# Value projections in another order with fewer loads, and weighted sums of 512 queries, in an encoder trunk

## The chip, the cores and the metric

The program runs on one core of one Trainium2 chip. The metric is the device time of one execution in microseconds; the median of several executions is compared. One execution was also taken with the hardware profiler.

## The reference

Two groups of 512 tokens (`x_prompt`, `x_sample`, 1024 wide) go through the same two layers and a final norm. All is float32.

```python
def trunk(x, ...):
    for i in range(DEPTH):                       # 2
        h = rms_norm(x, norm_g[i], NORM_EPS)
        if i % 2 == 0:
            x = x + diff_attention(h, ...)
        else:
            x = x + bidir_retention(h, ...)
    return rms_norm(x, final_norm_g, NORM_EPS)

def diff_attention(h, w_in, ..., w_out, lambda_init):
    q, k, v, gate = split(h @ w_in)              # 2048 each
    # 16 heads of 128 for q and k, rotated; 8 heads of 256 for v
    p = softmax(q k^T)                           # per head of 128, 512 x 512
    a = p[:, :, 0] - lam * p[:, :, 1]            # two score maps for each head of v
    o = rms_norm(a v, subln_g) * (1 - lambda_init)
    return (o * silu(gate)) @ w_out

def bidir_retention(h, w_in, decay_fwd, decay_bwd, subln_g, w_out):
    q, k, v, gate = split(h @ w_in)              # 1024, 1024, 2048, 2048; 8 heads
    o = retention(q, k, v, forward) + retention(q, k, v, backward)
    return (rms_norm(o, subln_g) * silu(gate)) @ w_out
```

## The kernel before

**Numbers.** Each operand of a matrix product is split in a high part (ACT casts it, `hi_of`, L557) and a low part (DVE subtracts, `lo_of`, L560). A product is three passes (`PASSES`): high by high, high by low, low by high.

**Projections.** Both groups are projected together by a seven-product scheme of the Strassen-Winograd kind: the products P1 to P7 need sums and differences of the four quarters of a block of weights, x(i, k) with i the half of the columns and k the half of the rows, and of the activations (`Bop`, made once a layer by `make_b`). A `Unit` does one head of q, k or gate: 12 matrix products for each of P1 to P7, from two loads of weights. A `Double` does four heads of v at once: each of P1 to P7 is 48 matrix products of 512 columns on four banks, and its weights come in two parts (kh = 0, 1). There are two Doubles in each layer. `prep` loads weights into the ring `raw` (four places of 512 KB), combines them on DVE (L874, into the ring `st`, three places) and writes high and low parts into the ring `ws` (seven places). `product` runs on PE (L909; a `Unit`'s is L775). `evac` takes finished banks away, with copies on ACT (`copies`) or sums on DVE (`sums`, L931; a `Unit`'s is L836); finished values go through the ring `os` (three places) to DRAM on POOL's DMA queue (`v4_done`). `product_order` lists the products of all units; the last product of a unit, its P4, called the tail, is done among those of the next unit.

**Attention.** 64 tiles (h, g, t): 8 heads, 2 groups, 4 tiles of 128 queries. `soften(i)` does scores (L1488), maxima (DVE), exponentials (ACT) and the combination of the two maps (L1515 to L1518; the little product L1516 on POOL). `transp(i)` turns the tile's weights (L1529) and copies them, split, to `aT`. `av(i)` multiplies two tiles' turned weights with the values: 24 products of 256 columns (L1549). `weigh` applies the gate and squares (L1133 to L1139), `weighed` turns the squares and sums them (L1146, `norm_cols`), and then owes the output products (`out_step`, L1222), which `fill` takes from the list `todo` and puts between the other work, holding `lag` of them back. A round of the loop does two tiles.

**Order.** Nothing runs in the order in which it is written. `Plan` records each operation with a cost, its engine and its dependencies; `arrange` then lays out all five engines' instruction streams with a model of the chip: fixed costs, a window of 24 operations on PE, and for loads a bus of `BUS` KB per us and a landing time of `LANDS` us behind it. PE takes the first operation in order that is ready. `SHIFTS` is a list of random shifts of due times around given points of model time, applied one after another. The streams are fixed once the program is built; waits at run time are by semaphore.

Of the kernel before, what the change touches and what calls it, by code (L numbers as in the profile page):

```python
# [11 lines left out]
F32R = mybir.dt.float32r  # L12
# [70 lines left out]
class Buf:  # L83
# [22 lines left out]
    (981.69, 16, 1, 0.5, 213021),  # L106
    (972.58, 16, 4, 0.2, 818872),
    (71.17, 4, 4, 1, 327647),
    (46.35, 30, 0.3, 0.5, 428238),
    (3.95, 16, 4, 0.2, 816114),  # L110
    (1418.22, 30, 2, 0.5, 114979),
    (980.04, 16, 0.3, 1, 262223),
    (1432.93, 8, 2, 0.5, 884958),
    (606, 16, 4, 0.2, 960304),
    (609.71, 8, 4, 1, 273225),
    (1356.88, 16, 4, 0.05, 845020),
    (989.5, 16, 2, 0.2, 638973),
    (612.92, 16, 1, 1, 46815),
    (72.51, 8, 1, 0.2, 526217),
    (450.87, 30, 0.3, 0.5, 454703),  # L120
    (10.89, 4, 2, 0.2, 253607),
    (38.39, 4, 4, 1, 547017),
    (591.0, 30, 1, 0.5, 946504),
    (1438.0, 30, 4, 1, 685051),
    (1213.45, 8, 2, 1, 20059),
    (1158.93, 4, 4, 0.5, 167471),
    (610, 8, 4, 1, 767523),
    (50.27, 30, 1, 0.2, 661035),
    (49.27, 16, 1, 0.5, 145307),
    (1148.95, 30, 1, 0.2, 13611),  # L130
    (50.17, 16, 2, 1, 934360),
    (990, 4, 4, 1, 712196),
    (205.71, 16, 4, 0.05, 504913),
    (1654.45, 8, 1, 1, 848736),
    (166.08, 16, 1, 0.5, 725028),
    (39.66, 30, 0.3, 0.5, 236895),
    (1702.12, 16, 4, 1, 699179),
    (1432.0, 30, 2, 1, 30820),
    (1455.0, 8, 1, 1, 107516),
    (555.83, 4, 0.3, 1, 8481),  # L140
    (420.74, 16, 1, 0.2, 779996),
    (47.14, 16, 2, 1, 720854),
    (1440.0, 30, 4, 0.05, 545299),
    (1436.0, 16, 2, 1, 586767),
    (1384.8, 30, 1, 1, 153335),
    (275.52, 16, 4, 0.2, 453470),
    (1451.0, 8, 4, 0.5, 325473),
    (1455.0, 16, 2, 1, 664587),
    (1344.14, 8, 1, 0.5, 202339),
    (982, 4, 2, 0.5, 759339),  # L150
    (7.48, 4, 2, 0.05, 180379),
# [12 lines left out]
    (591.0, 30, 1, 0.5, 799606),
    (1187.38, 16, 4, 0.5, 571367),
    (223.29, 30, 0.3, 1, 580948),
    (1219.2, 16, 4, 1, 277891),
    (1484.43, 30, 4, 0.2, 340160),
    (1451.0, 4, 4, 0.2, 841352),
    (1440.0, 8, 2, 0.2, 980674),  # L170
    (1224.53, 8, 4, 1, 713870),
    (322.59, 4, 4, 0.2, 303760),
    (530.6, 4, 2, 0.5, 984079),
    (975.58, 30, 2, 0.2, 810649),
    (281.94, 8, 4, 1, 893829),
    (1009.56, 8, 2, 0.2, 187674),
    (294.42, 16, 1, 0.2, 362693),
    (256.75, 16, 2, 1, 888439),
    (173.3, 8, 4, 1, 447949),
    (1323.22, 30, 4, 0.2, 217427),  # L180
    (1436.0, 30, 2, 1, 363003),
# [3 lines left out]
class Plan:  # L185
# [7 lines left out]
    BUS = 380.0  # L193
    LANDS = 2.3
# [62 lines left out]
    def arrange(self, starts, shift):  # L257
# [45 lines left out]
        while len(out) < n_ops:  # L303
# [88 lines left out]
def trunk_kernel(  # L392
# [463 lines left out]
    class Double:  # L856
# [4 lines left out]
        def __init__(self, w, c0, done):  # L861
            self.w, self.c0, self.done = w, c0, done
            self.ops, self.s, self.banks = {}, {}, {}

        def prep(self, op, kh):

            def x(i, k):
                r = raw_t([P, 2, S])
                src = self.w[self.c0 // 256 + 2 * i + kh, k].rearrange("p (k c) -> p k c", k=2)
                dma(lambda: r.t, lambda: src, [], [r], 512)  # L870
                return r
# [4 lines left out]
            if op in ("P1", "P2", "P4"):  # L876
                src = x(*dict(P1=(0, 0), P2=(0, 1), P4=(1, 1))[op])
# [37 lines left out]
        def evac(self, op):  # L915
# [11 lines left out]
            def sums(banks, cs):  # L927
                out = []
                for ps, c in zip(banks, cs):
                    e = e_t()  # L930
                    dve(S, lambda e=e, ps=ps, c=c: nc.vector.tensor_tensor(e.t, ps.t, c.t, op=ALU.add), [ps, c], [e])  # L931
                    out.append(e)
                return out
            if op == "P2":
# [1037 lines left out]
```

## Time and profile before

| | |
|---|---|
| median of 3 runs | 1716.92 us (1716.82 to 1718.17) |
| profiled execution | 1716.36 us |
| its span, first to last instruction | 1714.4 us |
| mean granted clock of TensorE | 0.999 |
| PE, DVE, ACT, POOL busy | 1698.0, 1477.5, 900.5, 365.7 us |
| matrix products | 8969 |
| moved by DMA | 349.64 MB |

Layer one's projections fill about the first 600 us, attention then goes to about 980, layer two's projections to about 1430, and retention to the end. Busy time counts execution alone, not waits or the issuing of DMAs; a product on PE is shown with its whole pipeline, so products overlap in the rows and their cost is the distance from start to start.

### The profile page before, as it was taken

The page shows a single profiled execution, that of the slowest core. Times are in us where ns is not written, and L with a number is a line of the kernel's source. Part 1 is how long each engine was busy: PE and PEld are TensorE (multiplying, and loading weights), DVE is VectorE, ACT ScalarE, POOL GpSimd, SP SyncE. Part 2 cuts the span into 40 slices and gives each one's busy share as a digit, 9 for nine tenths or more (in the row PEclk, how much of TensorE's full clock was granted, in tenths as well). Part 3 has the DMA queues.
Part 4 walks back from the last instruction along what each step waited for, and adds up shares of the span by engine and source line. Part 5 has one row for each costly group of instructions (what it writes and reads, how often), then busy time and mean ns, then how long its engine had stood idle before and what let it go on. Part 6 is the DMA issues. An engine that isn't in the chain of part 4 may idle for free.

```text
span 1714.4 us, 25502 instructions
## 1 busy us (share of the span) xinstructions
PE 1698.0 (99%) x8969; PEld 1511.8 (88%) x8969; DVE 1477.5 (86%) x2405; ACT 900.5 (53%) x1862; POOL 365.7 (21%) x656
## 2 busy tenths in 40 slices
PE   9999999999999999999999999999999999999998
PEld 7888888888888889999999888888888888999997
DVE  8979869988779799888888897777987797998988
ACT  8754434544444565555545876444544454544446
POOL 1112232212232212111111201123222321111114
PEclk9999999999999999999999999999999999999999
DMA  5445864556755795455543524475567569765652
GB/s 229 135 154 148 269 229 161 171 159 188 265 186 175 236 367 188 178 195 197 195 162 123 185 93 166 166 277 209 172 218 279 191 211 409 273 250 195 246 209 99
DMA packets 103928, 349.64 MB, mean 204 GB/s; under 512 B 14436, under 2 KB 15608, under 8 KB 103800
## 3 DMA queue, kind: packets, MB, share of 16 engines
q1 hardware_dynamic: 70448, 238.61, 38.8%
q0 software_dynamic: 33024, 109.08, 18.3%
q8 instruction: 70, 1.15, 0.3%
q14 instruction: 58, 0.48, 0.1%
q10 hardware_dynamic: 328, 0.34, 0.1%
HBM read 230.52 MB, written 117.44 MB: 203 GB/s over the span
## 4 chain that ended last, share of the span: by engine, by line
PE 87%; DVE 6%; DMA 3%; issue 2%; ACT 1%; POOL 1%; ACTq 0%; SPq 0%; DVEq 0%; POOLq 0%
PE pj L775 18%; PE pj L1222 18%; PE sc L775 10%; PE o L775 8%; PE pj L909 6%; PE o L1549 5%; PE sc L1488 5%; PE o L909 3%; PE sc L909 3%; PE o L1759 2%; PE tp L909 2%; DVE ws L560 1%; PE o L1767 1%; DMA qk<-os 1%; PE tp L1738 1%
## 5 line engine op out<-in xcount | busy, mean ns | idle before, releaser
L1222 PE MATMUL pj<-ws,arena 128*128 128x512 f32 x1542 | 358.5, 380 | 0.0
L1222 PEld LDWEIGHTS pj<-ws,arena 128*128 128x128 f32 x1542 | 283.7, 189 | 36.1
L775 PE MATMUL pj<-b,ws 128*128 128x512 f32 x1080 | 251.1, 380 | 0.0
L775 PEld LDWEIGHTS pj<-b,ws 128*128 128x128 f32 x1080 | 203.2, 189 | 28.6 <-ACT c L1030 0.3
L1228 DVE SCALAR_TENSOR_TENSOR b<-pj,pad,b 128x512 f32<-128x512 f32 (+1 forms) x257 | 190.0, 742 | 15.9 <-PE pj L1222 15.4
L557 ACT CAST ws<-st 128x512 fp32r<-128x512 f32 (+1 forms) x192 | 131.8, 691 | 106.9 <-PE pj L775 39.0
L553 POOL DMA_DIRECT2D qk<-os x192 | 102.6, 538 | 367.3 <-DVE os L560 313.7
L560 DVE TENSOR_TENSOR ws<-st,ws 128x512 fp32r<-128x512 f32 (+1 forms) x192 | 148.1, 776 | 37.4 <-ACT ws L557 33.0
L775 PE MATMUL sc<-arena,ws 128*128 128x512 f32 x768 | 176.9, 380 | 0.0
L775 PE MATMUL o<-arena,ws 128*128 128x512 f32 x744 | 170.3, 380 | 1.9 <-DVE arena L620 1.9
L557 ACT CAST ws<-raw 128x512 fp32r<-128x512 f32 (+2 forms) x165 | 125.7, 762 | 79.0 <-PE o L775 28.4
L775 PEld LDWEIGHTS sc<-arena,ws 128*128 128x128 f32 x768 | 144.8, 189 | 20.3
L560 DVE TENSOR_TENSOR ws<-raw,ws 128x512 fp32r<-128x512 f32 (+2 forms) x165 | 142.3, 864 | 20.4 <-ACT ws L557 17.0
L775 PEld LDWEIGHTS o<-arena,ws 128*128 128x128 f32 x744 | 139.9, 189 | 22.5 <-DVE arena L620 2.6
L775 PE MATMUL pj<-arena,ws 128*128 128x512 f32 x636 | 149.2, 380 | 0.0
L775 PEld LDWEIGHTS pj<-arena,ws 128*128 128x128 f32 x636 | 119.8, 189 | 17.1 <-DVE arena L560 0.2
L553 POOL DMA_DIRECT2D v<-os x128 | 91.9, 720 | 150.1 <-DVE os L560 99.3
L1506 ACT ACTIVATE b<-sc,pad 128x512 f32<-128x512 f32 x128 | 87.3, 691 | 51.8 <-DVE pad L1496 51.2
L557 ACT CAST os<-e 128x512 fp32r<-128x512 f32 x96 | 65.9, 686 | 82.5 <-DVE e L931 26.6
L1488 PE MATMUL sc<-arena 128*128 128x512 f32 x384 | 96.4, 386 | 0.0
L1549 PEld LDWEIGHTS o<-arena 128*128 128x128 f32 x768 | 90.8, 192 | 1.8
L1549 PE MATMUL o<-arena 128*128 128x256 f32 x768 | 91.0, 275 | 0.0
(251 smaller groups left out, 3040.0 us busy)
## 6 DMA issues: line engine op xcount, KB each, us to landing
qk<-os POOLq DMA_DIRECT2D x192, 256.0 KB, 4.6
arena<-qk SPq DMA_DIRECT2D x96, 512.0 KB, 6.0
raw<-in_da_w_in_dram SPq DMA_DIRECT2D x83, 512.0 KB, 5.1
raw<-in_ret_w_in_dram SPq DMA_DIRECT2D x68, 512.0 KB, 4.9
v<-os POOLq DMA_DIRECT2D x128, 256.0 KB, 2.9
arena<-v SPq DMA_DIRECT2D x64, 512.0 KB, 4.4
os<-g SPq DMA_DIRECT2D x32, 512.0 KB, 7.6
g<-e POOLq DMA_DIRECT2D x48, 256.0 KB, 2.7
```

The costliest lines, as they stand in the source:

```text
L553: plan.op(on, cost, lambda: q.dma_start(out(), in_()), r, w, lands=lands + kb / 200.0, kb=kb, load=any(isinstance(k[0] if isinstance(k, tu ...
L557: act(n, lambda: nc.scalar.copy(dst(), src()), r, w)
L560: dve(n, lambda: nc.vector.tensor_tensor(dst(), src(), hi().bitcast(F32), op=ALU.subtract), r, w)
L775: nc.tensor.matmul(ps.t, a[u][0]()[:, k, :], self.weave(bt[k][:, v, :]), start=(opens and k == 0 and i == 0), stop=(k == 3 and i == 2), sk ...
L909: nc.tensor.matmul(ps.t, bt[2 * kh + j][:, v, t * P:(t + 1) * P], woven(a[u][:, j, :]), start=(opens and kh + j + i == 0), stop=(kh == 1 a ...
L1222: nc.tensor.matmul(ps[:, here], o[a][:, e, t * P:(t + 1) * P], woven(u[b][:, e, :])[:, p * n // 2:(p + 1) * n // 2, :], start=(m == 0), st ...
L1228: axpy(n, lambda half=half, here=here, ps=ps: nc.vector.scalar_tensor_tensor(half, ps[:, here], rr[:, t % 2:t % 2 + 1], half, op0=ALU.mult ...
L1488: nc.tensor.matmul(s.t, q[:, a, t * P:(t + 1) * P], woven8(k[:, b, :]), start=(n == 0), stop=(n == 2))
L1506: act(840, lambda j=j, s=s, m=m: nc.scalar.activation(p[:, j, :], s.t, AF.Exp, bias=m.t, accum_out=sm[:, 2 * j + n:2 * j + n + 1]), [s, m] ...
L1549: nc.tensor.matmul(o[:, e * 256:(e + 1) * 256], v[b][:, j, e * P:(e + 1) * P], woven(aT[a][:, j, :]), start=(n == 0), stop=(n % 12 == 11), ...
L1738: nc.tensor.matmul(s[:, 0:256], kt[:, u, t * P:(t + 1) * P], woven(v_[v][:, t, :]), start=(j == 0 and i == 0), stop=(j == 1 and i == 2))
L1759: nc.tensor.matmul(o[:, e * 256:(e + 1) * 256], v_[v][:, 2 * c + j, e * P:(e + 1) * P], woven(a_[:, u, j * 256:(j + 1) * 256]), start=(e = ...
```

## The change

- In a `Double` the order of the products is P5, P1, P6, P7, P3, P2, behind the tail of the unit before, where it was P2, that tail, P1, P5, P6, P3, P7. Quarters x(0, 0) and x(0, 1) are loaded once and kept for their second and third use, and P7's difference is written over its own quarter: 6 loads for each part, 12 for a unit, where there were 18. Which bank sums are copied first follows the new order.
- In attention, ten blocks of four tiles (tiles 20 to 59) form the weighted sums for all 512 queries at once (`av4`: two banks, 12 products of 512 columns each) and turn the squares of four tiles together (`weighed4`). The tiles before and after go on by twos. `aT` now holds four tiles; to make room, the keys of group 0 go to the ring `st`. No output products are held back from tile 20 on.
- The planner's model: from 40 us of model time on, loads land 1.0 us later and the bus is slower. `SHIFTS` is another list (45 entries for 76).

```diff
-    BUS = 380.0
-    LANDS = 2.3
+    BEGINNING = 40.0
+    BUS = {True: 380.0, False: 360.0}
+    LANDS = {True: 2.3, False: 3.3}
...
-                bus = max(bus, at + cost) + kb / self.BUS
-                end = max(at + cost + lands, bus + self.LANDS)
+                early = at < self.BEGINNING
+                bus = max(bus, at + cost) + kb / self.BUS[early]
+                end = max(at + cost + lands, bus + self.LANDS[early])
...
-            def x(i, k):
-                r = raw_t([P, 2, S])
-                src = self.w[self.c0 // 256 + 2 * i + kh, k].rearrange("p (k c) -> p k c", k=2)
-                dma(lambda: r.t, lambda: src, [], [r], 512)
-                return r
+            def x(i, k, again=False):
+                if not again:
+                    r = self.x[i, k, kh] = raw_t([P, 2, S])
+                    src = self.w[self.c0 // 256 + 2 * i + kh, k].rearrange("p (k c) -> p k c", k=2)
+                    dma(lambda: r.t, lambda: src, [], [r], 512)
+                return self.x[i, k, kh]
...
-                src = x(*dict(P1=(0, 0), P2=(0, 1), P4=(1, 1))[op])
+                src = x(*dict(P1=(0, 0), P2=(0, 1, True), P4=(1, 1))[op])
...
-                src = combine(self.s[kh], self.s[kh], x(0, 0), ALU.subtract)
+                src = combine(self.s[kh], self.s[kh], x(0, 0, True), ALU.subtract)
...
-                a, b = x(0, 0), x(1, 0)
-                src = combine(st_t([P, 2, S]), a, b, ALU.subtract)
+                a, b = x(0, 0, True), x(1, 0)
+                src = combine(b, a, b, ALU.subtract)
...
-            if op == "P2":
-                s["c1"] = copies(Y, c_t)
+            if op == "P5":
+                s["c5"] = copies(Z, e_t)
             elif op == "P1":
-                self.done(0, 0, sums(X, s["c1"]))
-            elif op == "P5":
-                s["c5"] = copies(Z, c_t)
+                s["c1"] = copies(X, c_t)
             elif op == "P6":
                 s["c2"] = copies(X, m_t)
+            elif op == "P7":
+                self.done(1, 1, sums(X, s["c5"]))
             elif op == "P3":
                 self.done(0, 1, sums(Z, s["c2"]))
-            elif op == "P7":
-                self.done(1, 1, sums(X, s["c5"]))
+            elif op == "P2":
+                self.done(0, 0, sums(Y, s["c1"]))
...
-                out += [(u, "P2"), tail] + [(u, op) for op in ("P1", *SEQ[2:-1])]
+                out += [tail] + [(u, op) for op in ("P5", "P1", "P6", "P7", "P3", "P2")]
...
-        t = slot(i, [P, 2, S], F32R, shift)
+        t = work("st", [P, 2, S], 3, F32R) if i is None else slot(i, [P, 2, S], F32R, shift)
...
+    def four(i):
+        return 20 <= i < N - NT
+
+    def av4(i):
+        h, g, t = tiles[i]
+        aT, v = st[i]['aT'], vt[h, g]
+        settle(h - 1, g)
+        oT[h, g] = new_oT(g)
+        os_, sqs_ = [bank("o") for _ in range(2)], []
+        for e in range(2):
+            o = os_[e]
+            def fn(e=e, o=o):
+                n = 0
+                for a, b in PASSES:
+                    for j in range(NT):
+                        nc.tensor.matmul(o.t, v[b][:, j, e * P:(e + 1) * P], woven(turned_aT(a)[:, j, :]),
+                                         start=(n == 0), stop=(n == 11))
+                        n += 1
+            pe(2.592, fn, [*aT[0], *aT[1], *v], [o])
...
+        dve(S, lambda: nc.vector.tensor_tensor(sqs_[0].t, sqs_[0].t, sqs_[1].t, op=ALU.add), sqs_, [sqs_[0]])
+
+    def weighed4(i):
...
...
-        lag = max(0, min(LAG, i // 2 - 5))
+        lag = max(0, min(LAG, i // 2 - 5)) if i < 20 else 0
         fill(2, lag)
         if i == FIRST:
             transp(i - 1)
         soften(i + 1)
         fill(2, lag)
-        at(av, i - 2, N)
+        last = i == N - 2
+        if last:
+            weighed4(i - 6)
+        if i % NT == 0 and four(i - NT):
+            av4(i - NT)
+        elif not four(i - 2):
+            at(av, i - 2, N)
         at(transp, i, N)
         at(transp, i + 1, N)
-        at(weighed, i - 4, N)
+        if not last and i % NT == 2 and four(i - 6):
+            weighed4(i - 6)
+        elif not four(i - 4):
+            at(weighed, i - 4, N)
         fetch_next(i)
```

More of the change, by code (lines that the diff above doesn't have):

```diff
@@ L121 @@
[L121 to L151, printed above, removed]
@@ L167 @@
[L167 to L181, printed above, removed]
+    (986, 8, 4, 1, 93064),
@@ new lines @@
+    (610, 8, 4, 1, 773508),
+    (69.47, 30, 2, 1, 966209),
+    (11.95, 8, 0.3, 0.2, 913846),
+    (61.49, 8, 1, 1, 169919),
+    (1440.0, 16, 4, 1, 460894),
+    (60.89, 4, 1, 0.5, 766918),
+    (611.01, 4, 4, 0.5, 90366),
+    (60.49, 8, 1, 0.5, 615480),
+    (11.49, 16, 1, 0.05, 997522),
+    (594.5, 16, 4, 0.2, 897486),
+    (594.0, 4, 4, 0.5, 516104),
+    (171.2, 16, 2, 1, 114794),
+    (71.73, 30, 1, 0.5, 280256),
+    (1692.71, 8, 1, 0.5, 658398),
+    (1423.43, 30, 2, 0.05, 47590),
+    (11.99, 16, 0.3, 0.05, 523605),
@@ new lines @@
+    (1423.39, 30, 1, 1, 258131),
+    (542.13, 8, 2, 0.5, 679735),
+    (11.49, 16, 0.3, 1, 785172),
+    (1415.16, 30, 4, 0.05, 143263),
+    (1052.6, 30, 2, 0.5, 712630),
+    (1425.39, 30, 1, 0.5, 612061),
+    (1421.39, 16, 2, 0.5, 937799),
+    (1440.0, 16, 4, 0.2, 433253),
+    (1432.0, 8, 2, 0.2, 226625),
+    (1439.5, 16, 2, 0.5, 224311),
+    (167.17, 30, 0.3, 1, 538302),
+    (60.85, 8, 4, 0.2, 501862),
+    (971.85, 16, 2, 0.2, 92752),
+    (988, 30, 2, 0.2, 682172),
+    (323.89, 30, 1, 0.5, 421681),
@@ L182 @@
+    (1116.51, 8, 4, 1, 475762),
+    (1438.0, 16, 4, 1, 181843),
+    (556.93, 4, 4, 0.2, 876751),
+    (88.32, 16, 2, 0.2, 123322),
+    (1453.0, 16, 4, 0.05, 400133),
+    (330.06, 4, 4, 1, 373302),
+    (1053.14, 16, 4, 1, 11164),
+    (417.08, 4, 2, 1, 803091),
+    (1364.17, 8, 2, 1, 473008),
+    (1455.0, 16, 2, 0.5, 320260),
+    (9.9, 4, 0.3, 0.5, 859533),
+    (11.49, 8, 1, 1, 64754),
+    (10.01, 16, 0.3, 0.2, 125826),
 )
@@ L1200, in out_weights, with out_step @@
         wsn[h, i] = (hi, lo)
-    def out_step(w, h, g, t, i, o, rr, last, parts=1):
+    def out_step(w, h, g, t, i, o, rr, last, parts=1, whole=False):
         owed[h, g] -= 1
@@ L1225, in fn @@
                         m += 1
-            pe(1.3 / parts, fn, [(o[0], t // 2), (o[1], t // 2), *u], [ps])
+            pe(1.3 / parts, fn, [*((a, t // 2) for a in o), *u] if not whole else [*o, *u], [ps])
             half = x[:, i * S + p * n:i * S + (p + 1) * n]
@@ L1232, in out_step, with owe @@
                 last(g, t, i, half, n, part, i == 1 and p == parts - 1)
-    def owe(w, h, g, t, o, rr, last):
+    def owe(w, h, g, t, o, rr, last, whole=False):
         for i in range(2):
@@ L1237, in owe @@
             parts = 2 if w is wo2 and (h, g, t, i) == (NH - 1, NG - 1, NT - 1, 1) else 1
-            todo.append(lambda i=i, parts=parts: out_step(w, h, g, t, i, o, rr, last, parts))
+            todo.append(lambda i=i, parts=parts: out_step(w, h, g, t, i, o, rr, last, parts, whole))
     def settle(h, g):
@@ L1523, in transp @@
     def transp(i):
-        p, n = st[i]['p'], i % 2
-        tp = bank("pj" if n else "tp", "tpa")
+        p = st[i]['p']
+        tp = bank("pj" if i % 2 else "tp", "tpa")
         def fn():
@@ new lines, in weighed4, with fn @@
+    def weighed4(i):
+        h, g, t = tiles[i]
+        sq, (ps, jk) = st[i]['sq'], st[i]['o']
+        def fn():
+            for n in range(NT):
+                nc.tensor.transpose(ps[:, n * P:(n + 1) * P], sq[:, n * P:(n + 1) * P], ident.t)
+        pe(0.44, fn, [sq, ident], [ps])
+        for c in range(2):
+            ss, rr, sm = col(2, "css"), col(2, "crr", 9), st[i + 2 * c]['sm']
+            for n in range(2):
+                act(P + 120, lambda n=n, c=c, ss=ss: nc.scalar.activation(
+                    jk[:, (2 * c + n) * P:(2 * c + n + 1) * P], ps[:, (2 * c + n) * P:(2 * c + n + 1) * P], AF.Copy,
+                    accum_out=ss[:, n:n + 1]), [(ps, 2 * c + n)], [(jk, 2 * c + n), (ss, n)])
+            pool(60, lambda sm=sm, ss=ss: nc.gpsimd.tensor_tensor(ss.t, ss.t, sm[:, 2:4], op=ALU.add), [ss, sm], [ss])
+            pool(200, lambda ss=ss, rr=rr: nc.gpsimd.tensor_tensor(rr.t, ss.t, mhalf[:, 0:2], op=ALU.pow),
+                 [ss, mhalf], [rr])
+            for n in range(2):
+                owe(wo1, h, g, 2 * c + n, oT[h, g], rr, finished, True)
@@ L1538, in av @@
     def av(i):
         h, g, t = tiles[i]
-        aT, v = st[i]['aT'], vt[h, g]
+        aT, v = st[i - t % NT]['aT'], vt[h, g]
         o = bank("o")
+        here = slice(t * P, (t + 2) * P)
         def fn():
```

75 lines of the change are left out of this document (32 added, 43 removed).

## The prediction

> **What bounds the kernel now.** I read the page's busy shares first, then the table of stretches, then the waits of TensorE (PE), and last the order of time in the stages that the change touches.
>
> ```profile
> PE 1698.0 (99%) x8969; PEld 1511.8 (88%) x8969; DVE 1477.5 (86%) x2405; ACT 900.5 (53%) x1862; POOL 365.7 (21%) x656
> ...
> 0.00:50.00 50.00, 45.44 (x237) 38.50 (x238) 43.93 (x95) 40.59 (x78) 6.42 (x13) 1.00 0.50 197
> 700.00:750.00 50.00, 50.00 (x310) 45.98 (x309) 43.70 (x77) 25.29 (x69) 8.35 (x22) 1.00 0.45 169
> 1700.00:1714.00 14.00, 7.02 (x39) 6.13 (x37) 8.63 (x17) 10.26 (x29) 7.66 (x9) 0.89 0.57 218
> ```
>
> The columns of a stretch are its length, busy us (instructions) of PE, weight load, DVE, ACT and POOL, the granted clock, the DMA share and GB/s. PE is busy for 1698.0 of 1714.4 us; 4.6 us are missing in the first 50 us and 7.0 behind the last product. In mid-attention it is never idle, at full clock. So only two things shorten this program: less time on PE, or the few waits in the middle. DVE has 43.7 of 50 us there, so a schedule that bunches DVE work can put PE back.
>
> ```profile
> PE o L775 <- DVE arena L620: 1.9, 2, 1.7
> PE tp L1738 <- DMA arena<-v: 1.5, 1, 1.5
> PE sc L909 <- DVE ws L560: 1.4, 2, 0.7
> ...
> PE sc L1384 <- ACT b L540: 0.8, 1, 0.8
> ...
> PE tp L1529 <- DVE b L1518: 0.5, 1, 0.5
> ```
>
> Total us, times, longest. These are the waits that a new order can reach: 1.9 in the start of layer one, 0.5 at the start of attention (L1529), 0.8 at the start of layer two (L1384), 1.4 in the value units (L909), 1.5 at the start of retention (L1738).
>
> **Part 1: weighted sums of 512 queries.** One round of attention (two tiles of 128 queries) in order of time on PE:
>
> ```profile
> 704.97 1.54 PE L1488 MATMUL sc<-arena 128*128 128x512 f32 x6
> 706.35 2.75 PE L1222 MATMUL pj<-ws,arena 128*128 128x512 f32 x12
> 708.94 1.46 PE L1488 MATMUL sc<-arena 128*128 128x512 f32 x6
> 710.23 2.75 PE L1222 MATMUL pj<-ws,arena 128*128 128x512 f32 x12
> 712.82 2.84 PE L1549 MATMUL o<-arena 128*128 128x256 f32 x24
> 715.50 0.60 PE L1529 MATMUL tp<-ident,b 128*128 128x128 f32 x4
> 715.94 0.60 PE L1529 MATMUL pj<-ident,b 128*128 128x128 f32 x4
> 716.38 0.38 PE L1146 MATMUL o<-ident,m 128*128 128x128 f32 x2
> 716.51 1.54 PE L1488 MATMUL sc<-arena 128*128 128x512 f32 x6
> ```
>
> Durations overlap, so the cost of a group is the distance to the next start. Twelve products of 512 columns take 712.82 - 710.23 = 2.59 us, 215.8 ns each; twenty-four of 256 take 715.50 - 712.82 = 2.68 us, 111.7 ns each. A block of four tiles needs 48 narrow ones now, 5.36 us, and 24 wide ones after, 5.18: 0.18 us less, 1.80 us in ten blocks. The last is off PE's own path, since PE is what never rests here. The count of transposes for the row norms stays four a block, so does that of the squares and copies; two DVE sums of 256 columns become one of 512. All that is off PE, and DVE's 6 us of rest in 50 cover it: zero.
>
> The Trainium skill, page "TensorE: Matmul & The Clock Gate", section "Back-to-back issue gap", gives 262 cycles for 256 columns and 518 for 512; by that a block would save 48 x 109.2 - 24 x 215.8 = 62 ns, an estimate, and ten blocks 0.6 us instead of 1.8. The rows above put 111.7 ns on the narrow product, beyond the page's figure, and the rows decide.
>
> What moves with it: the turned weights of four tiles share one set of places, so the copies out of the next transposes wait until the sums end. They wait for that now too, and the sums stand ahead of the transposes in both orders: zero. The keys of group 0 move from the arena into the ring "st". Their first load must wait for the ring's last readers in layer one:
>
> ```profile
> L560 DVE TENSOR_TENSOR ws<-st,ws x6: 689/696/719, 560.9 to 581.6; 128x512 fp32r<-128x512 f32 x6
> ```
>
> (the readers of "st" around the change of stage, first and last start), and, in order of time and from the DMA issues, the first scores and a load's time to landing:
>
> ```profile
> 593.07 1.46 PE L1488 MATMUL sc<-arena 128*128 128x512 f32 x6
> ...
> arena<-qk SPq DMA_DIRECT2D x96, 512.0 KB, 6.0
> ```
>
> The ring's last reader starts at 581.6, a load lands in 6.0, and the first scores start at 593.1: 5 us to spare, zero; if the load takes the 11 us that crowded ones do (9.81 in Part 2), it is up to 0.5 us once. Later keys are asked for four tiles after their places fell free.
>
> **Part 2: the value units.** The four Doubles compute the same seven products. Each part drops three of nine loads, six per unit: 24 loads, 12.6 MB.
>
> The DMA issues, with KB and us to landing, and one crowded load from the chain:
>
> ```profile
> raw<-in_da_w_in_dram SPq DMA_DIRECT2D x83, 512.0 KB, 5.1
> raw<-in_ret_w_in_dram SPq DMA_DIRECT2D x68, 512.0 KB, 4.9
> ...
> 1270.86 9.81 DMA raw<-in_ret_w_in_dram
> ```
>
> PE in order of time at P5 of the two Doubles of layer two, then the chain and DVE's order of time before the first of these waits:
>
> ```profile
> 1129.26 1.89 PE L909 MATMUL sc<-ws,arena 128*128 128x512 f32 x8
> 1131.89 3.72 PE L909 MATMUL sc<-ws,arena 128*128 128x512 f32 x16 [0.74 <-DVE ws L560]
> ...
> 1297.17 1.89 PE L909 MATMUL sc<-ws,arena 128*128 128x512 f32 x8
> 1299.76 2.42 PE L909 MATMUL sc<-ws,arena 128*128 128x512 f32 x10 [0.70 <-DVE ws L560]
> ```
>
> ```profile
> 1120.50 8.15 DMA qk<-os
> ...
> 1123.05 0.67 DVE L931 TENSOR_TENSOR e<-pj,c 128x512 f32<-128x512 f32 x1
> 1125.18 1.23 DVE L874 TENSOR_TENSOR st<-raw,raw 128x1024 f32<-128x1024 f32 x1 [0.73 <-DMA raw<-in_ret_w_in_dram]
> 1129.41 0.69 DVE L560 TENSOR_TENSOR os<-e,os 128x512 fp32r<-128x512 f32 x1 [0.53 <-ACT os L557]
> 1130.62 1.22 DVE L560 TENSOR_TENSOR ws<-st,ws 128x1024 fp32r<-128x1024 f32 x1
> ```
>
> The loads as such are worth nothing on PE: SP's queue and the transfers lie beside it. The waits are worth something. Eight products from 1129.26 end their turn at 1130.99, and the next starts at 1131.89: 0.90 us. The other Double: 1297.17 + 1.73 = 1298.90 against 1299.76: 0.86. Together 1.76. Both sit in P5 and have one story. A store of the rope unit before (8.15 us) holds an output buffer; ACT and then DVE queue behind it; DVE does a sum, and only then the low part that P5's second half needs. In the 20.7 us of P1 and P5 (96 products of 215.8 ns) DVE has P1's own sums and low parts, 4 x (0.67 + 0.69) = 5.4, the preparation of P5 and P6, 2 x 2 x (1.23 + 1.22) = 9.8, beside the rope unit's rotation and stores. In the new order P5, P1 and P6 leave only copies on ACT; the first sums come after P7. In P5 and P1 together DVE then prepares P1 (2 x 1.22) and P6 (4.9), 7.3 us instead of 15.2, before the same rotation. So I take the whole 1.76; the ends are 0 (it moves to another product) and 1.76, plus a loss from the moved tail (rival 2). The later sums meet 2 x 1.22 to 4.9 us of preparation per 10.4 us of product, 5.4 + 4.9 = 10.3 at the most, for one product only.
>
> **Part 3: landings.** BUS and LANDS only steer the order that the planner writes; no instruction changes its price. They assume loads 1.0 us later and a slower bus beyond 40 us, and the list of shifts is another. Where PE now waits for a transfer, 1.5 us at L1738, the planner would see it coming; it may give back between 0 and 1.5, and I take half, 0.75, since the first loads of retention are short of bus and not of order. The waits at L775, L1384 and L1529 are for DVE and ACT, not for loads: a new order may take them away or lengthen them alike, 0 taken, 3.2 us the end below, as much the end above.
>
> **Sum.** -1.80 - 1.76 - 0.75 = -4.31 us against the profiled execution's own 1716.36 us (its span is 1714.4, 1.96 lie around it): 1712.05. That execution is 0.56 under the median of the runs, 1716.92; against the median the sum gives 1712.6.
>
> **Rivals.** A difference under about 0.2%, 3.4 us, is none that the measurement can tell: faster is below 1713.5, slower above 1720.4.
>
> 1, better: the new order also loses the other half of 1.5 and the 3.2 us of waits for DVE and ACT: 1712.6 - 0.75 - 3.2 = 1708.6. For it: they are single events, not a law of the kernel. Against: the start of layer one has DVE at 43.9 of 50 us, and work that DVE must do first isn't ordered away.
>
> 2, no change that can be told: the value units' waits move. Each Double now puts the tail, the unit before's P4, right behind that unit's P7, and P4 adds into the bank that DVE must first have read: a sum of 0.67 us (L931), and its way there and back, taken as the 0.3 us by which 0.90 exceeds it. Four units at 0.67 to 0.97 us give 2.7 to 3.9 back, if no part of P5 is put between; P5 also opens with four loads where P2 opened with two. Then the time is 1712.6 + 2.7 to 3.9 = 1715.3 to 1716.5; if only the 1.76 doesn't come, 1714.4. Against: P5's operands lie ready as early as the ring of seven allows, and the planner may pass P4 over.
>
> 3, slower: the second round of each block. With no sums between, the turns of the odd tile come too soon:
>
> ```profile
> 712.52 1.21 DVE L560 TENSOR_TENSOR ws<-raw,ws 128x1024 fp32r<-128x1024 f32 x1
> 713.98 0.75 DVE L1518 SCALAR_TENSOR_TENSOR b<-b,pad 128x512 f32<-128x512 f32 x1 [0.25 <-POOL pad L1516]
> ...
> 709.47 0.34 POOL L1516 TENSOR_SCALAR pad<-pad,pad 128x1 f32<-128x1 f32 x1 [2.07 <-DVE pad L1515]
> 712.71 1.24 POOL L1516 TENSOR_SCALAR pad<-pad,pad 128x1 f32<-128x1 f32 x1 [2.89 <-DVE pad L1515]
> ```
>
> The odd tile's scores are issued by 710.23, its weights are combined at 713.98 + 0.75 = 714.73, 4.5 us later. Between lie 2.59 us of output products and 0.44 of the even tile's turns, 3.03: 1.46 us short, where 2.68 us of sums fill it now. The next scores (1.29) can be put between, which leaves 0.17 uncovered. But POOL's little product took 0.34 us once and 1.24 beside a DVE operation with two inputs, and the planner reckons one price for it, so its order can be wrong by 0.9. At 0.9 to 1.46 us in ten blocks the kernel loses 9.0 to 14.6: 1721.6 to 1727.2. It decides above 0.78 us a block. Against: eight output products of a block (1.3 us each, 2.59 for two above) are at hand in the round, and any of them put between covers the whole lack.
>
> The Trainium skill's page "SBUF — State Buffer", section "Who interferes with whom", says that a DVE instruction with two SBUF inputs contends with a GpSimd instruction that reads SBUF, and that the loser blocks for the whole of it. The pair of 1.24 and 1.21 above agrees with it; by that rule this rival's place recurs wherever those two meet.
>
> **How the numbers follow.** Forecast 0.48, at 1712.6, its own range 1711 to 1714, of which I put 0.43 below 1713.5. Rival 1: 0.17. Rival 2: 0.25. Rival 3: 0.10, 0.07 of it beyond the bound and 0.03 where part of the loss only eats the gain. Faster 0.43 + 0.17 = 0.60; same 0.05 + 0.25 + 0.03 = 0.33; slower 0.07. The range goes from rival 1's 1708.6 to the upper end of rival 2 and a little over, 1716.8; rival 3 and the tails of the others stay out.
>
> **What would show it.** The weighted sums: 240 products of 512 columns at a distance of 215.8 ns, 288 narrow ones left, 8969 - 240 = 8729 products in all. The loads: 71 and 56 instead of 83 and 68, 349.6 - 12.6 = 337.0 MB. PE's wait at the value units for "ws" gone; a wait of "pj" for DVE "e" at the Doubles would be rival 2. A wait of the turns (now L1529) that comes ten times would be rival 3. PE's busy time should fall by about 1.8 us; if the time falls by more than 5, the waits at the edges of the stages did it and my second or third part is too small. The prediction is wrong if PE gets new waits of over 0.3 us a block in attention.

## The result, and the profile after

The changed kernel takes 1708.26 us (median of 4 runs, 1708.21 to 1708.48), the kernel before 1717.55 beside it (4 runs, 1716.82 to 1719.92): a ratio of 0.9946, interval 0.993 to 0.9962, faster by 9.3 us. The forecast was 1712.6, faster by 4.3; the range ended at 1708.6. The profiled execution took 1708.25 us, its span is 7.9 us shorter than before.

The page of the kernel after: spans, busy time, bytes, and two lines of its DMA issues.

```profile
span 1706.5 us, 24879 instructions
...
PE 1695.6 (99%) x8729; PEld 1504.9 (88%) x8729; DVE 1478.3 (87%) x2394; ACT 906.1 (53%) x1863; POOL 359.5 (21%) x656
...
DMA packets 100469, 337.02 MB, mean 197 GB/s; under 512 B 14052, under 2 KB 15224, under 8 KB 100344
...
raw<-in_da_w_in_dram SPq DMA_DIRECT2D x71, 512.0 KB, 4.1
...
raw<-in_ret_w_in_dram SPq DMA_DIRECT2D x56, 512.0 KB, 4.1
```

8729 products, 71 and 56 loads, 337.02 MB: all as counted ahead. PE's busy time fell by 1698.0 - 1695.6 = 2.4 us, and its idle time (span less busy) from 16.4 to 10.9, by 5.5. So less than a third of the gain is work left out; the rest is waiting left out. Where the waiting was is read from the stretches (length, busy us of PE, weight load, DVE, ACT and POOL, clock, DMA share, GB/s), before:

```profile
50.00:100.00 50.00, 50.00 (x233) 43.57 (x232) 48.67 (x82) 37.40 (x65) 7.62 (x14) 1.00 0.51 168
150.00:200.00 50.00, 50.00 (x233) 43.79 (x232) 43.08 (x64) 21.82 (x33) 11.39 (x22) 1.00 0.65 196
600.00:650.00 50.00, 49.47 (x302) 44.83 (x301) 45.64 (x84) 32.57 (x80) 9.58 (x23) 1.00 0.87 345
950.00:1000.00 50.00, 49.08 (x269) 43.40 (x268) 45.11 (x72) 43.39 (x103) 8.24 (x13) 1.00 0.45 164
1100.00:1150.00 50.00, 49.26 (x232) 42.92 (x232) 41.06 (x55) 23.80 (x35) 15.19 (x24) 1.00 0.85 299
1250.00:1300.00 50.00, 49.30 (x236) 43.14 (x235) 44.75 (x67) 22.42 (x32) 13.02 (x22) 1.00 0.71 236
1400.00:1450.00 50.00, 48.41 (x290) 43.66 (x289) 38.63 (x67) 28.53 (x61) 10.21 (x19) 1.00 0.99 373
```

and after:

```profile
0.00:50.00 50.00, 47.60 (x246) 40.97 (x247) 44.16 (x95) 40.72 (x78) 6.99 (x13) 1.00 0.51 197
50.00:100.00 50.00, 49.52 (x230) 43.10 (x229) 48.79 (x82) 37.80 (x67) 8.13 (x15) 1.00 0.51 179
150.00:200.00 50.00, 49.37 (x229) 43.01 (x228) 49.99 (x72) 23.21 (x33) 12.61 (x24) 1.00 0.67 200
600.00:650.00 50.00, 49.92 (x308) 45.20 (x307) 44.67 (x81) 30.21 (x76) 9.65 (x23) 1.00 0.88 337
950.00:1000.00 50.00, 50.00 (x278) 44.77 (x277) 44.58 (x71) 45.09 (x103) 7.71 (x13) 1.00 0.47 169
1100.00:1150.00 50.00, 50.00 (x236) 43.68 (x235) 38.80 (x52) 23.56 (x33) 13.72 (x22) 1.00 0.57 184
1250.00:1300.00 50.00, 50.00 (x241) 44.12 (x240) 44.65 (x63) 24.28 (x34) 11.51 (x20) 1.00 0.65 211
1400.00:1450.00 50.00, 50.00 (x311) 45.94 (x311) 40.48 (x70) 29.18 (x63) 9.15 (x15) 1.00 1.00 389
```

Idle is length less PE's busy time. It fell by 2.16 us in the first 50 us, 0.45 at the start of attention, 0.92 at the start of layer two, 0.74 and 0.70 at its two Doubles, 1.59 at the start of retention, and rose by 0.48 at 50 to 100 us and by 0.63 at the first Double, 150 to 200. All other stretches up to the last product agree within 0.05. The sum is -5.45. The waits of PE after (total us, times, longest):

```profile
PE sc L1327 <- DVE pad L547: 1.2, 1, 1.2
PE pj L752 <- DVE e L813: 0.6, 1, 0.6
PE sc L1386 <- ACT b L517: 0.5, 1, 0.5
PE sc L1386 <- DVE b L519: 0.5, 1, 0.5
PE pj L752 <- DVE ws L537: 0.5, 1, 0.5
```

L1327 and L1386 are the first products of the program, as before. None of the listed waits of before in the middle is left, the DMA wait at retention's start among them, and attention has no new one. Two are new: L752 on L537, 0.48 us at 63 us, and L752 on L813, which is rival 2's, the moved tail. PE in order of time, at that tail and at a weighted sum:

```profile
179.72 1.46 PE L887 MATMUL sc<-ws,arena 128*128 128x512 f32 x6
181.81 2.86 PE L752 MATMUL pj<-b,ws 128*128 128x512 f32 x12 [0.63 <-DVE e L813]
...
720.79 5.34 PE L1538 MATMUL o<-arena 128*128 128x512 f32 x24
725.97 0.60 PE L1505 MATMUL tp<-ident,b 128*128 128x128 f32 x4
```

The sums of four tiles take 725.97 - 720.79 = 5.18 us, as worked out ahead.

### The profile page after: what moved, and what is told of

The parts are those of the page before. It is cut to its first block, busy times and chain, and to the rows that moved or that the text cites. A ratio compares the mean times of both kernels' runs of the same rounds, so it can differ in the third digit from the quotient of the medians.

```text
span 1706.5 us, 24879 instructions
## 1 busy us (share of the span) xinstructions
PE 1695.6 (99%) x8729; PEld 1504.9 (88%) x8729; DVE 1478.3 (87%) x2394; ACT 906.1 (53%) x1863; POOL 359.5 (21%) x656
## 2 busy tenths in 40 slices
DMA packets 100469, 337.02 MB, mean 197 GB/s; under 512 B 14052, under 2 KB 15224, under 8 KB 100344
## 4 chain that ended last, share of the span: by engine, by line
PE 94%; DVE 4%; issue 1%; POOL 1%; ACT 0%; DMA 0%; POOLq 0%; DVEq 0%; ACTq 0%
PE pj L752 20%; PE pj L1197 18%; PE sc L752 10%; PE o L752 8%; PE pj L887 7%; PE sc L1464 5%; PE o L887 4%; PE sc L887 4%; PE o L1538 3%; PE o L1805 3%; PE tp L887 2%; PE o L1585 2%; PE o L1813 1%; PE sc L1760 1%; PE tp L1784 1%; PE pj L1505 1%
## 5 line engine op out<-in xcount | busy, mean ns | idle before, releaser
L752 PE MATMUL pj<-b,ws 128*128 128x512 f32 x1080 | 251.2, 380 | 1.1 <-DVE e L813 0.6
L752 PEld LDWEIGHTS pj<-b,ws 128*128 128x128 f32 x1080 | 203.5, 189 | 30.0 <-DVE e L813 1.0
L537 DVE TENSOR_TENSOR ws<-raw,ws 128x512 fp32r<-128x512 f32 (+2 forms) x173 | 152.3, 884 | 41.9 <-PE tp L887 21.5
L752 PE MATMUL sc<-arena,ws 128*128 128x512 f32 x768 | 177.2, 380 | 0.0
L537 DVE TENSOR_TENSOR ws<-st,ws 128x512 fp32r<-128x512 f32 (+1 forms) x184 | 138.7, 759 | 44.1 <-ACT ws L534 35.8
L534 ACT CAST ws<-st 128x512 fp32r<-128x512 f32 (+1 forms) x184 | 123.7, 675 | 97.7 <-PE pj L752 40.2
L534 ACT CAST ws<-raw 128x512 fp32r<-128x512 f32 (+2 forms) x173 | 133.8, 775 | 68.2 <-PE o L752 22.8
L752 PE MATMUL o<-arena,ws 128*128 128x512 f32 x744 | 169.2, 380 | 0.0
L752 PEld LDWEIGHTS sc<-arena,ws 128*128 128x128 f32 x768 | 144.8, 189 | 20.0
L752 PEld LDWEIGHTS o<-arena,ws 128*128 128x128 f32 x744 | 140.4, 189 | 19.7
L752 PE MATMUL pj<-arena,ws 128*128 128x512 f32 x636 | 148.7, 380 | 0.0
L752 PEld LDWEIGHTS pj<-arena,ws 128*128 128x128 f32 x636 | 120.3, 189 | 16.8
L1472 DVE TENSOR_REDUCE pad<-sc 128x1 f32<-128x512 f32 x128 | 83.5, 684 | 4.2 <-PE sc L1464 4.1
L887 PE MATMUL pj<-ws,b 128*128 128x512 f32 x360 | 81.0, 379 | 0.0
L887 PEld LDWEIGHTS pj<-ws,b 128*128 128x128 f32 x360 | 68.2, 189 | 9.5
L805 ACT COPY c<-pj 128x512 f32<-128x512 f32 x72 | 42.0, 586 | 64.8 <-PE pj L752 60.0
```

Source lines behind the costliest of these rows:

```text
L534: act(n, lambda: nc.scalar.copy(dst(), src()), r, w)
L537: dve(n, lambda: nc.vector.tensor_tensor(dst(), src(), hi().bitcast(F32), op=ALU.subtract), r, w)
L752: nc.tensor.matmul(ps.t, a[u][0]()[:, k, :], self.weave(bt[k][:, v, :]), start=(opens and k == 0 and i == 0), stop=(k == 3 and i == 2), sk ...
L887: nc.tensor.matmul(ps.t, bt[2 * kh + j][:, v, t * P:(t + 1) * P], woven(a[u][:, j, :]), start=(opens and kh + j + i == 0), stop=(kh == 1 a ...
L1472: dve(S, lambda s=s, m=m: nc.vector.tensor_reduce(m.t, s.t, op=ALU.max, axis=AX.X, negate=True), [s], [m])
```

## The experiments

Each kernel tried is the one before or the changed one with the edits named. A list of shifts fits one plan alone: where the instructions or the planner's model were changed, a new list was searched for the shortest time by the planner's own reckoning ("refit", 13 to 32 entries). So a kernel's whole time mixes its edit with its list. That is why each is read by place, and why several kernels differ by the list alone. Idle PE time, in us, worked out from the stretches of each profile as above:

| kernel | time, median (range) | ratio to before | 20-50 us | Doubles | attention's start | layer two's start | retention's start |
|---|---|---|---|---|---|---|---|
| before | 1717.55 | 1 | 1.78 | 1.44 | 0.53 | 0.92 | 1.59 |
| changed | 1708.26 | 0.9946 | 0.00 | 0.63 | 0.08 | 0.00 | 0.00 |
| refit_all | 1717.7 (1715.2-1720.4) | 0.9997 [0.9988, 1.0006] | 0.03 | 2.81 | 1.46 | 2.19 | 0.95 |
| refit_all_2 | 1711.67 (1711.3-1712.2) | 0.9962 [0.9948, 0.9977] | 0.18 | 2.38 | 0.17 | 0.11 | 0.04 |
| change_no_list | 1715.99 (1714.3-1720.0) | 0.9992 [0.9983, 1.0001] | 0.19 | 3.50 | 0.20 | 0.11 | 0.97 |
| refit_old_landings | 1712.12 (1711.5-1714.9) | 0.9969 [0.9958, 0.9981] | 0.00 | 0.57 | 0.16 | 1.64 | 1.16 |
| refit_narrow_sums | 1712.25 (1711.3-1714.9) | 0.9964 [0.9951, 0.9977] | 0.03 | 3.24 | 0.01 | 0.13 | 0.00 |
| refit_old_units | 1712.03 (1711.2-1713.0) | 0.9962 [0.9947, 0.9977] | 2.69 | 0.00 | 0.20 | 1.15 | 0.03 |
| before_refit | 1719.04 (1716.6-1721.8) | 1.001 [1.0, 1.0019] | 1.21 | 2.99 | 1.46 | 0.01 | 1.47 |
| before_new_landings | 1715.14 (1713.8-1718.2) | 0.9987 [0.9977, 0.9996] | 1.84 | 2.49 | 0.63 | 0.59 | 0.13 |
| all_loads | 1715.57 (1713.3-1719.6) | 0.9987 [0.9978, 0.9996] | 2.65 | 0.41 | 0.20 | 1.16 | 0.17 |
| before_fair_due | 1721.03 (1718.3-1722.0) | 1.0017 [1.0008, 1.0027] | 0.32 | 4.25 | 1.99 | 2.18 | 1.79 |
| before_fair_new_landings | 1711.59 (1711.5-1714.3) | 0.9966 [0.9953, 0.9979] | 0.00 | 0.88 | 0.63 | 0.12 | 0.09 |
| old_units_fair | 1711.1 (1711.0-1711.5) | 0.9959 [0.9945, 0.9973] | 0.31 | 1.20 | 0.08 | 1.68 | 0.04 |
| change_fair | 1711.05 (1711.0-1711.8) | 0.9961 [0.9946, 0.9976] | 0.31 | 0.90 | 0.07 | 1.65 | 0.04 |
| change_fair_2 | 1709.09 (1708.8-1710.5) | 0.995 [0.9936, 0.9965] | 0.07 | 0.65 | 0.00 | 0.47 | 0.04 |
| tail_later | 1708.46 (1707.9-1708.6) | 0.9949 [0.9934, 0.9964] | 0.00 | 0.35 | 0.08 | 0.00 | 0.00 |
| copy_later | 1715.07 (1713.7-1716.9) | 0.9986 [0.9977, 0.9996] | 0.03 | 1.59 | 1.58 | 2.19 | 1.60 |

(Doubles: 150 to 250 and 1050 to 1350 us; the starts: 550 to 650, 950 to 1050, 1350 to 1450. Not in the columns: up to 3.6 us in the first 20, up to 2.2 at 50 to 100, 0.93 at 250 to 550 in all_loads, under 0.3 elsewhere up to 1690.) Three theories were held: A, the later landings give what was gained beyond the forecast; B, the list does; D, formed after the second batch, the twelve loads do, by way of the planner.

**The change in parts, each with a refit list.** refit_all is the changed kernel with only `SHIFTS` replaced. refit_old_landings also undoes the landings, refit_narrow_sums the wide sums, refit_old_units the value units' order and loads.

```diff
 # refit_old_landings
-    BUS = {True: 380.0, False: 360.0}
-    LANDS = {True: 2.3, False: 3.3}
+    BUS = {True: 380.0, False: 380.0}
+    LANDS = {True: 2.3, False: 2.3}
 # refit_narrow_sums (and lag, last as before)
     def four(i):
-        return 20 <= i < N - NT
+        return False
```

> The changed kernel with another list of shifts, found by a search of ten minutes on the planner's own reckoning (18 entries). Control for the other three, whose lists were found in the same way. Theory A (the gain beyond 4.3 us comes from the later landings in the planner, which keep PE out of waits for loads): 1708 +- 1 us, no wait for a DMA over 0.5 us between 600 and 1650 us. Theory B (it comes from the particular list of 45 entries that fitted): 1710 to 1713, other waits of 0.5 to 1.5 us at the edges of the stages.

> The changed kernel with BUS 380 and LANDS 2.3 throughout, as before, and a list found for it by the same search; both changes of the instructions stay. Theory A: 1711 to 1713, 3 to 5 us over the control, with waits behind late loads at the edges of the stages (about 1130, 1300, 1430, 610 us) of some 3 to 4 us together. Theory B, or that the value units' new order alone removed those waits: within 1 us of the control.

> The changed kernel with weighted sums of 256 queries throughout (no block of four tiles, output products held back as before), new value units and new landings, a list found for it by the same search. By my Part 1: 1.8 us over the control, all of it PE busy time, no new wait in attention. If the wide sums also loosened something else: 2.5 or more over.

> The changed kernel with the value units' old order and 18 loads, wide sums and new landings, a list found for it by the same search. By my Part 2 (their waits go because DVE has less to do between P1 and P5): 1.1 to 1.8 us over the control with a wait of PE for the low part of P5 at about 1130 and 1300. By theory A (late loads that the planner did not see): no wait there, and under 1 us over the control besides what the planner itself reckons with in layer one (2.8 in all by its reckoning).

The whole change with another list is no faster than before, 1717.7; each of the three with a part undone is faster than it, by 5.4 to 5.7 us. Each of the three had been expected at this control or slower. So a comparison of whole times says nothing of the parts, and B holds at least this far: the list decides as much as the whole change. By place two things are plain: the wait at 44 us came back only in refit_old_units, and a DMA wait at the start of retention only in refit_old_landings.

**The same instructions with no list and with a second refit list.** change_no_list empties `SHIFTS`; refit_all_2 is a second search.

> The changed kernel with an empty list of shifts: the planner's plain order with the later landings. Theory A (landings give the robustness, the list only the last 2.5 us that the planner itself reckons): 1710.5 to 1712. Theory B (the list of 45 entries is a lucky fit): over 1713, with waits at the edges that the planner did not reckon with.

> The changed kernel with a second list found by a shorter search with other random numbers: the scatter between lists for the same instructions and the same landings. Theory B: 1710 to 1718, a wait of 2 to 3 us at 195 us (behind a store of the unit before) as likely as not, since three of five kernels with the new order have shown it. If the list of 45 entries is nothing special: 1708 to 1710, and no wait over 1 us after the first 100 us.

One set of instructions and one planner's model thus gave 1708.26, 1711.67, 1715.99 and 1717.7 us: a scatter of 9.4, as large as the gain.

**The kernel before, with a refit list, and with the new landings too.**

> The kernel before, instructions and landings unchanged, with another list of shifts, found by a search of seven minutes on the planner's reckoning (25 entries for 76). Theory B (each list leaves other waits, whatever the instructions): within 3 us of the kernel before on either side, the waits at 1130, 1300 and 1431 us gone or moved. Theory A (the short landings make them): the waits at 1130, 1300 and 1431 stay, 1715 to 1718.

> The kernel before, instructions unchanged, with the later landings of the change and a list found for it by the same search (24 entries). Theory A: the waits at 1130, 1300 and 1431 us gone (1.0 + 1.0 + 2.3 of lost time), the start as it was: 1712.5 to 1714. Theory B: anything from 1713 to 1720, a wait of over 1 us at some other edge.

A fresh list alone gave the old kernel nothing (1719.04). With the new landings it came to 1715.14, and the idle time at retention's start fell from 1.47 to 0.13. The waits in layer two's value units did not go, though A had expected it; they moved to the next product (1.07 and 1.41 us). A wait for a load at retention's start with the old landings, then the stretch around it in that kernel and in before_new_landings:

```profile
1417.85 0.91 PE L1737 MATMUL sc<-arena 128*128 128x256 f32 x6 [0.92 <-DMA arena<-qk]
```

```profile
1400.00:1450.00 50.00, 48.84 (x296) 44.11 (x295) 39.63 (x68) 28.73 (x63) 9.30 (x18) 1.00 1.01 388
1400.00:1450.00 50.00, 49.87 (x289) 44.91 (x288) 40.44 (x70) 29.33 (x61) 11.12 (x20) 1.00 1.01 385
```

The DMA engines are as busy in both. Over all rows of the table the new landings leave no wait for a DMA at retention's start, and the old ones always do: 1.5 us in before, 0.5, 1.2 and 0.9 in before_refit, before_fair_due and refit_old_landings. (The 0.95 to 1.60 that refit_all, change_no_list and copy_later show there wait for ACT or DVE.) Two waits for keys at the start of attention, in refit_all and copy_later (1.5 and 1.6), stand beside new landings, so they don't cure every place.

**The loads.** Before the change a Double has 18 loads. The planner takes an operation's due time from what follows it, less its own cost; for a load this cost holds the whole landing, 6.2 us by its reckoning, and it is subtracted along the ring of places too, where a load only has to start after another. 18 x 6.2 = 111 us then stand against 336 products, 73 us, and the shortfall is handed back to all DVE work that frees a place, down to 22 us into the program. There DVE's order differs between the two kernels, though what is listed up to 161 us is the same, and what PE waits for at 44 us, part of `make_b`, is pushed back. 12 loads make 74 us and next to no shortfall. That is D. Two edits test it from both sides: load again without need, or count only the issue along the ring.

```diff
 # all_loads: the changed kernel with 18 loads
-                if not again:
+                if True:
 # before_fair_due, before_fair_new_landings, old_units_fair, change_fair, change_fair_2
-            at = min((late[s] for s in succs[n]), default=None)
-            at = min(recent[n] + 20.0, now + 10.0) if at is None else at - cost
+            at = min((late[s] - (min(costs.values()) if n in ops[s][3] else cost)
+                      for s in succs[n]), default=None)
+            at = min(recent[n] + 20.0, now + 10.0) if at is None else at
```

> The changed kernel (value units in the new order, wide sums, later landings), but each quarter of the weights is loaded anew at every use, 18 loads a Double as before; a list found for it by the search of ten minutes. Theory D: the six loads that a Double saves act 130 us earlier, through the planner's due times. There every load of the ring of four counts 6.2 us behind the one before, 18 of them 111 us against 73 us of products, so what feeds the loads looks overdue from 22 us on and is put ahead of the work that PE waits for at 44 us (and again at 980 in layer two). D expects PE's wait for DVE at 44 to 46 us back (1 to 2 us) and 0.5 to 1.5 us at 974 to 1000, no other difference to the other lists for the changed kernel. Rival (the order of the products, or the list, freed the start): no wait at 44 us.

> The kernel before, all instructions, loads and landings unchanged; in the planner a load whose only tie to the next is its place in the ring no longer counts its landing in the next one's due time. A list found for it by the same search. Theory D: the wait at 44 to 46 us (1.0 to 2.1 us in all four kernels with 18 loads so far) falls under 0.6 us, that at 970 to 1000 under 0.5; the waits at the value units and at 1430 us, which have other causes, are as the list makes them. Rival: the wait at 44 us is as it was.

PE in order of time with all_loads:

```profile
41.19 0.66 PE L1335 MATMUL tp<-ident,b 128*128 128x128 f32 x4 [0.72 <-DVE arena L573]
...
46.80 3.50 PE L728 MATMUL o<-arena,ws 128*128 128x512 f32 x15 [1.93 <-DVE arena L573]
```

and its stretch from 20 to 50 us:

```profile
20.00:50.00 30.00, 27.35 (x142) 23.61 (x141) 29.39 (x54) 25.71 (x48) 4.25 (x5) 1.00 0.26 102
```

The same product in before_fair_due, and the same stretch:

```profile
45.03 5.23 PE L713 MATMUL o<-arena,ws 128*128 128x512 f32 x23 [0.32 <-DVE arena L558]
```

```profile
20.00:50.00 30.00, 29.68 (x154) 25.92 (x153) 30.00 (x55) 25.52 (x48) 4.50 (x5) 1.00 0.23 91
```

With 18 loads the wait is back (2.65 us idle) in a kernel that otherwise is the changed one; with 18 loads and the corrected due times it is all but gone (0.32) in a kernel whose instructions are those of before. Over the table: 18 loads with the old due times, five kernels, 1.21 to 2.69 us; all others, thirteen, 0.00 to 0.32. Each of these kernels has a list of its own, so it is this pattern over all lists that carries D, for this place. DVE is as busy in both (29.39 and 30.00 of 30 us), so it is the order of its work and not the amount. The wait at layer two's start did not follow: before_fair_due has 2.18 us there against an expectation that it would be gone too.

> As the run before this one, with the later landings too: the instructions of the kernel before under both corrections of the planner. If D and the landings are what freed the edges of the stages (start, 980, 1430), this kernel loses under 1 us more there than the changed one, and the rest of its distance is 1.8 us of narrow sums and what the value units wait: 1711 to 1713.5. If the edges were freed by the chosen list: 1714 to 1718.

> Old value units (old order, 18 loads) with the wide sums, the later landings and the corrected due times; a list found by the search of ten minutes. Theory D (the new units matter only through the due times): the starts of the layers as in the changed kernel, no wait over 1 us at 44 or 980 us, 1708.5 to 1711. If the new order is needed for itself: over 1712.

> The changed kernel with corrected due times and a list found by the same search. Theory D: the correction has little left to give here, since 12 loads count 74 us against 73 us of products: 1708 to 1711, with the usual scatter of lists; a wait of the tail at 181 us of 0.6 to 0.9 stays.

> The same with another list (other random numbers): 1708 to 1711. If it beats 1708.3 the changed kernel's own list is not the best that is to be had.

before_fair_new_landings has the instructions of before, every load and every product, and comes to 1711.59: 6.0 us below before, where the change gave 9.3, without its edits to the computation. old_units_fair and change_fair differ in the value units alone and share one list: 1711.1 and 1711.05. Once the due times are right, the new order and the twelve loads are worth nothing that can be measured with this list. Both still wait at layer two's start (1.68 and 1.65 us), where D had expected no wait over 1.

**The tail, and the wait at the Doubles.** tail_later moves the tail in front of the first Double, in the finished plan, behind the second piece of P5; copy_later is refit_all with one output copy (ACT, DVE, two stores) moved later.

```diff
+        tail, behind = 692, 708                                   # tail_later
+        moved, behind = [(629, "ACT"), (630, "DVE"), (631, "POOL"), (632, "POOL")], 720   # copy_later
```

> The changed kernel with its own list and order; only the tail in front of the first value unit stands one piece of six products later on PE, behind the second piece of P5. If the 0.9 us lost at 181 us is the wait of P4 for the bank that DVE reads (rival 2): that wait goes and the span is 0.6 to 0.9 us shorter, 1707.5. If DVE, busy 49.99 of 50 us there, is the real bound: a wait of the same size turns up within the next 20 us and nothing is won.

> The refitted kernel that waits 2.2 us at 195 us (1717.7), same list and order but for one output copy of the unit before the first Double: its halves on ACT and DVE, with their two stores, stand behind the weights' high part on ACT and four DVE operations that stood behind them. If DVE's 3.05 us at 182 us behind a store of 8.6 us made the wait: both are gone, and with them the throttled clock behind the wait (some 2.5 us): 1712 to 1714. If DVE simply has too much to do there: the wait stays over 1.5 us.

With the tail moved its wait is gone, and PE waits at the next half product instead:

```profile
193.25 1.89 PE L893 MATMUL pj<-ws,arena 128*128 128x512 f32 x8
195.49 2.86 PE L893 MATMUL pj<-ws,arena 128*128 128x512 f32 x12 [0.35 <-DVE ws L543]
```

The start-to-start distance of the eight, 2.24 us, is 0.51 over their 1.73. DVE was busy for 49.99 of 50 us there in the changed kernel (43.08 before): it is late as a whole. About half of the wait came back there, and the time is the same, 1708.46. In the profiled execution PE was 0.57 us behind the changed kernel's before the tail (177.71 against 177.14) and 0.29 behind the Double's P1 (204.22 against 203.93), so the move won about 0.3 us by place, which the start of the program hid.

In refit_all the wait sits at the step from P5 to P1. From its chain, then from the order of time of ACT, DVE and PE, then two stretches:

```profile
175.64 8.59 DMA qk<-os
```

```profile
184.34 0.66 ACT L507 CAST os<-e 128x512 fp32r<-128x512 f32 x1 [4.77 <-DMA qk<-os]
...
185.03 0.83 DVE L510 TENSOR_TENSOR os<-e,os 128x512 fp32r<-128x512 f32 x1 [3.05 <-ACT os L507]
...
197.88 8.00 PE L860 MATMUL pj<-ws,arena 128*128 128x512 f32 x28 [2.19 <-DVE ws L510]
205.71 2.54 PE L860 MATMUL tp<-ws,arena 128*128 128x512 f32 x11
```

```profile
195.00:200.00 5.00, 2.81 (x11) 2.08 (x10) 5.00 (x6) 2.68 (x3) 1.05 (x2) 0.89 0.42 105
200.00:205.00 5.00, 5.00 (x19) 4.11 (x19) 5.00 (x8) 1.76 (x4) 1.05 (x2) 0.77 0.58 166
```

A store of the rope unit takes 8.59 us and holds a place of `os`; ACT stands behind it for 4.77 and DVE behind ACT for 3.05. DVE is then full, and some 12 us later PE waits for the low part. DVE and PE in copy_later, and a stretch of it:

```profile
187.08 0.85 DVE L514 TENSOR_TENSOR os<-e,os 128x512 fp32r<-128x512 f32 x1 [1.85 <-ACT os L511]
...
196.99 3.29 PE L864 MATMUL pj<-ws,arena 128*128 128x512 f32 x14 [1.00 <-DVE ws L514]
```

```profile
200.00:205.00 5.00, 5.00 (x25) 4.38 (x24) 4.97 (x8) 2.43 (x5) 1.04 (x2) 1.00 0.76 236
```

1.20 us less on DVE are 1.19 less on PE, and the clock stays at 1.00; the whole is 1715.07 against 1717.7. Both waits were expected to go, for 1712 to 1714; about half of each is left. That is the chain of the prediction's Part 2, at another product. The other kernels with the new order agree: in the four where ACT stands behind such a store for 4.3 to 5.1 us (refit_all, refit_all_2, refit_narrow_sums, change_no_list), PE waits 1.72 to 2.83 us at this step; in the other seven ACT waits 0.9 us at most, and PE 0 to 1.00.

## Why the prediction was wrong, by its steps

**Part 1 was right.** The products and their distance came as worked out: 5.18 us a block for 5.36, 1.80 in ten. (By the Trainium skill's figures, page "TensorE: Matmul & The Clock Gate", section "Back-to-back issue gap", 0.6 us of it would have been left, an estimate; the rows held.) Rival 3 did not come: attention has no wait in the changed kernel.

**Part 2: the size came near by luck, its cause did not hold.** The 1.76 at the two Doubles of layer two went in full (the stretches' 1.44 of idle, and the gaps around it that a product's modelled end hides). Against it stand 0.63 at the first Double, where rival 2's tail happened once in four units at its price, so about 1.1 net. The stated reason, that DVE has half as much to do beside P5 and P1, fails. DVE was not less busy there but more: 18.2 and 18.6 us around these two products before (193.97 to 214.69 and 1118.89 to 1140.62 us, layers one and two), 21.1 and 20.2 in 21.1 and 21.2 us after (182.80 to 203.93 and 1104.30 to 1125.47). And refit_old_units has the old order and no idle time at the Doubles, refit_all the new one and 2.81 us. What decides at the step from P5 to P1 of the first Double is where a crowded store lands among the output copies, and that follows from the planner's order; for the other places this is not shown.

**"The loads as such are worth nothing on PE" is the first step that failed.** On the chip it holds: old_units_fair and change_fair take the same time. But a load is also an entry in the planner's due times, and six loads more for a Double move DVE's work in the plan over 100 us ahead of them. That was the wait at L775, 1.78 us of idle, taken at 0. The prediction let the planner's model steer the order in Part 3, but costed the removed loads on their queue alone.

**Part 3 was sized at half.** All of the 1.52 at L1738 went (1.59 idle), not 0.75. The reason given for half, that retention's first loads are short of bus and not of order, is refuted: the DMA share there is 1.00 after, 0.99 before, at a higher rate (389 against 373 GB/s), and there is no wait. "0 taken" for L1384 and L1529 was the third: 0.92 and 0.45 went. For these two no edit is shown to be the cause; with other lists the same instructions have 0.00 to 2.19 at layer two's start.

Together the waits away from the Doubles gave 1.59 + 0.92 + 0.45 + 2.16 - 0.48 = 4.64 us of idle where 0.75 stood, 3.9 more; the tail took 0.63 back. That leaves 3.3 of the 3.6 by which the span fell further than forecast. The prediction had named this case: with more than 5 us, the waits at the edges of the stages did it, and its second or third part was too small. Rival 1 described it, for 1708.6, and was held at 0.17 by the sentence "work that DVE must do first isn't ordered away". It was ordered away: all_loads and before_fair_due show it at L775.

**What no step had** is the spread of the list. The four versions of one set of instructions span 9.4 us, so a forecast of this kernel from its instructions alone carries that much, and the own range, 1711 to 1714, was too narrow for it. What share of the gain is the list's stays open: with the other lists the changed kernel lies between 0.9962 and 0.9997 of before, 0.5 to 6.5 us below it, and only with its own list, which leaves no wait over 0.7 us between 20 us and the last product, by 9.3. These distances hold the lists on both sides; they are no price of landings, loads and sums by themselves. How that list was chosen isn't in the kernel. No version tried beats the changed kernel; tail_later equals it.

## What to carry to other kernels

Where a planner writes the order, removing work from an engine or queue that isn't the bottleneck can still pay, through the due times: ask what each removed operation does to them, and whether a cost that overlaps (a landing, a ring of places) is added up as if it were serial. Judge a part by the wait at its own place, not by the whole time of two plans: here two plans of the same work differed by up to 9.4 us. An engine that is busy for 99% of the span can still win from the last 1%, wait by wait, and single waits that look like accidents are ones that another order may not have.

## What the runs showed of the hardware

A short wait of PE can cost more than itself. In refit_all, 28 products after the wait of 2.19 us take 205.71 - 197.88 = 7.83 us, where 28 x 215.8 ns are 6.04: 1.8 us more, with the granted clock at 0.89 and 0.77 of full speed in the two stretches above, 19 products in the 5 us that hold 25 in copy_later. The clock fell in seven places of five kernels, this one among them, after waits of 2.11 to 2.83 us before runs of 512 columns, down to 0.65 in a stretch of 5 us; eleven waits of 1.52 to 1.94 us left the clock at 1.00, and so did one of 2.18 before a short transpose. The Trainium skill, page "TensorE: Matmul & The Clock Gate", section "What's actually happening", puts the fall of the clock after an idle window of about 3.4 us; in these runs it came with less, so in this kernel the waits over 2 us are worth removing first.
